# A one-core decoder step: three weight sums leave stage 1, the scalings after the mixing get a tile of their own, a batch's first weights and up's first operands change place

## The chip, the cores and the metric

One core of one Trainium2 chip runs the whole step as one program. The metric is the device time of that program in microseconds (us). TensorE (PE) does the matrix products, VectorE (DVE), ScalarE (ACT) and GpSimd (POOL) the elementwise work, and all transfers are issued by the queue of SyncE (SP). Each engine works through its own list of instructions strictly in order.

## The reference

One layer of a decoder for a prompt of 2048 positions and 8 samples of 8 positions (2112 columns, width 1024). Cut to what matters here:

```
h     = rms_norm(x, pre_mix_g)
z     = h @ w_in                      # q, k, v, sg_u, sg_v, mq, gate_logits
...                                   # three branches of width 512: windowed attention,
                                      # spatial gating, attention into 256 memory tokens
proj  = einsum('blnc,ncd->blnd', branches, w_o)
mixed = sum(sigmoid(gate_logits) * proj, axis=branch)
x     = x + rms_norm(mixed, post_mix_g)
up    = rms_norm(x, pre_ffn_g) @ w_up            # width 2 * 2816
c     = conv_b + causal convolution of width 3 over up
act   = gelu(c[:2816]) * c[2816:]
x     = x + rms_norm(act @ w_down, post_ffn_g)
```

Everything is float32, and so is the accuracy that is wanted: each operand of a product is split into a rounded part and a rest, and three products of parts (rounded with rounded, rounded with rest, rest with rounded) make one.

## The kernel before

The work lies feature-major: 128 features on the partitions, positions along the free axis. **Stage 1** (`pass_a`, 0 to about 470 us, and `pass_b`, about 470 to 714 us) makes the three branches, pair of token blocks by pair of token blocks, and writes them to the tensors `br`. **Stage 2** goes through the 2112 columns in three groups g of 704 (two halves of 352): `gate_phase` (714 to 1248 us) makes the gates, 12 jobs per group; `mix_phase` (to 1553 us) makes the output projection, with 24 products of 128 x 704 per group (3 branches n, 8 output tiles o), multiplies each by its gate and adds them up; `up_phase` (to 2467 us) has 22 jobs per group, `down_phase` the rest.

Gate, up and down use a Strassen-like scheme: a job is a 256-row block of the weights times a group, and takes 7 products of 12 matmuls (128 x 128 by 128 x 352) instead of 8. For that each job wants seven weight tiles: three blocks as they are (wa11, wa12, wa22) and four sums of blocks (ws1 to ws4). `eng.weights` loads raw blocks (`r..`, line 824), and splits them: ACT casts the rounded part (L76), DVE subtracts it to get the rest (L77). The sums are made once, by DVE (L113 in `prep_sums`, L837 where a gate job makes its own), split, written to `sum_d` (L116, L848) and read back where they are wanted. The group's columns are likewise split by `eng.operands`: 8 tiles of 704 columns are loaded (L781), scaled by norm and gain (L783), and give seven sets of four operand tiles (ob11, ot1, ob21, ot2, ob22, ot3, ot4), with differences on DVE (L793) and splits on ACT and DVE.

The sums that up needs, 22 blocks f of `w3`, are made ahead: `prep_sums` for f below NF1 = 14 runs in `pass_b`, two per item, with a pool of two buffers for the split sums; f = 14 to 21 run in gate's groups 1 and 2, in every third job. Those of down (d0 to d7) run in up.

In `mix_phase` a product `ps_p` has three buffers in PSUM. DVE evicts it, multiplied by its gate (L1038 for the first branch, into `m`; L1041 for the others, into `sl`, added to `m` by POOL, L1042). When group g is done, `post_mix` runs during group g + 1: the norm `rs` (L997), then for each of 8 tiles a scaling of `m` in place (L1004, DVE), `x` reloaded as `xr` (two buffers, L1003) and added by POOL (L1007), the sum written to `x1_d` (L1008), its square on ACT (L988) added up on DVE (L989). After the last group, `up_phase` begins with the norm of group 0 and the operands `u0`, made under `tc.high_priority(None)`, which puts them ahead of all other work that is ready.

The order on each engine is set when the program is built, by a scheduler that goes through the code with a model of the time and with priorities; code that is written earlier, or marked with a priority, is placed earlier. Tile pools of a later phase lie on memory of an earlier one, and wait for its tiles.

## Time and profile before

| | before |
|---|---|
| median of 3 runs | 2978.36 us (2975.37 to 2981.42) |
| profiled execution, its own time | 2972.76 us |
| its span | 2970.9 us |
| PE busy | 2868.4 us (97%) |
| DVE busy | 2057.4 us (69%) |
| ACT busy | 1395.8 us (47%) |
| POOL busy | 499.2 us (17%) |
| granted TensorE clock, mean | 0.984 |

The profiled execution lies 5.6 us under the median, and 1.9 us of it lie outside the span. A busy share counts an instruction from its start to its end, at whatever clock. What a stretch lost for PE is its length less its busy time weighted with the granted clock: at a clock of 0.50 (TensorE at 1.2 instead of 2.4 GHz) a busy microsecond is worth half of one.

### The profile page before, as it was taken

How to read it: one execution, taken by the hardware profiler on the slowest of the kernel's cores; microseconds unless marked ns; L12 is line 12 of the kernel's file. 1: busy time of each engine (PE TensorE's matmuls, PEld its weight loads, DVE VectorE, ACT ScalarE, POOL GpSimd, SP SyncE). 2: the span in 40 equal slices, each digit the busy share in tenths (PEclk: the TensorE clock that was granted, in tenths of full speed). 3: DMA queues.
4: the chain of work that ended last, by engine and by line, in shares of the span. 5: the costliest groups of instructions: out<-in, count | busy, mean ns of one | idle time of the engine just before them, and what ended most of it. 6: DMA issues, size and time to landing. Idle time of an engine off the chain costs nothing.

```text
span 2970.9 us, 52583 instructions
## 1 busy us (share of the span) xinstructions
PE 2868.4 (97%) x19340; PEld 2821.0 (95%) x19340; DVE 2057.4 (69%) x3901; ACT 1395.8 (47%) x2793; POOL 499.2 (17%) x576
## 2 busy tenths in 40 slices
PE   8999999996999999999999999999999999999997
PEld 8998998996999999999989999999999999999997
DVE  6676567888767353468787777867785667767667
ACT  5555556334555354423325555555554454334333
POOL 3221100010000000035552211311242121000000
PEclk9999999998999999999999999999999999999998
DMA  6123223887889999867678987898787778576674
GB/s 213 52 68 88 73 69 115 266 294 269 326 309 350 340 358 342 319 222 247 207 270 297 336 327 245 309 335 328 241 321 244 242 241 287 198 271 230 210 268 134
DMA packets 310945, 732.32 MB, mean 247 GB/s; under 512 B 37968, under 2 KB 90192, under 8 KB 310672
## 3 DMA queue, kind: packets, MB, share of 16 engines
q1 hardware_dynamic: 310688, 728.97, 70.5%
q8 instruction: 153, 2.51, 0.3%
q14 instruction: 104, 0.85, 0.1%
HBM read 553.55 MB, written 176.27 MB: 246 GB/s over the span
## 4 chain that ended last, share of the span: by engine, by line
PE 87%; DVE 4%; DMA 4%; issue 2%; ACT 2%; POOL 1%; SPq 0%; DVEq 0%; ACTq 0%; POOLq 0%
PE ps_xu L885 17%; PE ps_xg L885 9%; PE ps_yu L885 9%; PE ps_p L1029 8%; PE ps_xd L885 6%; PE ps_yg L885 5%; PE ps_p L1285 5%; PE ps_wu L885 4%; PE ps_q L215 3%; PE ps_yd L885 3%; PE ps_mqp L229 3%; PE ps_wg L885 2%; PE ps_kv L215 2%; PE ps_sv L215 2%; PE ps_wd L885 1%
## 5 line engine op out<-in xcount | busy, mean ns | idle before, releaser
L1170 DVE SCALAR_TENSOR_TENSOR c<-e,k_conv_w,c 128x704 f32<-128x704 f32 (+1 forms) x264 | 252.0, 956 | 109.6 <-ACT c L1166 104.0
L1029 PE MATMUL ps_p<-b,w_p 128*128 128x352 f32 x1728 | 285.4, 327 | 11.7 <-DVE m L1038 9.0
L1029 PEld LDWEIGHTS ps_p<-b,w_p 128*128 128x128 f32 x1728 | 281.9, 191 | 13.1 <-issue 9.5
L885 PE MATMUL ps_xu<-ot_u,ws_u 128*128 128x352 f32 x1584 | 275.3, 323 | 0.0
L885 PEld LDWEIGHTS ps_xu<-ot_u,ws_u 128*128 128x128 f32 x1584 | 257.2, 188 | 0.0
L1042 POOL TENSOR_TENSOR m<-m,sl 128x704 f32<-128x704 f32 x48 | 105.4, 2204 | 653.4 <-DMA bx<-br 574.3
L77 DVE TENSOR_TENSOR wa_u<-r_u,wa_u 128x512 fp32r<-128x512 f32 x198 | 138.8, 704 | 24.4 <-ACT wa_u L76 22.0
L1166 ACT ACTIVATE c<-e,k_conv_b,k_conv_w 128x704 f32<-128x704 f32 (+1 forms) x132 | 129.6, 982 | 50.5 <-DVE e L1145 39.5
L885 PE MATMUL ps_xg<-ot_h,ws_g 128*128 128x352 f32 x864 | 152.0, 324 | 0.0
L76 ACT CAST wa_u<-r_u 128x512 fp32r<-128x512 f32 x198 | 123.1, 624 | 61.4 <-PE ps_yu L885 44.1
L885 PE MATMUL ps_xu<-ob_u,wa_u 128*128 128x352 f32 x792 | 149.0, 323 | 0.5 <-ACT sq_m L988 0.5
L1157 POOL COPY tails<-e 128x2 f32<-128x2 f32 x88 | 71.5, 813 | 456.5 <-DVE e L1145 446.4
L885 PE MATMUL ps_yu<-ot_u,ws_u 128*128 128x352 f32 x792 | 142.8, 325 | 3.9 <-DVE sl L1041 3.9
L885 PE MATMUL ps_wu<-ob_u,wa_u 128*128 128x352 f32 x792 | 146.6, 323 | 0.0
L885 PEld LDWEIGHTS ps_xg<-ot_h,ws_g 128*128 128x128 f32 x864 | 141.5, 188 | 0.2 <-ACT ws_g L76 0.2
L1285 PE MATMUL ps_p<-a,wd 128*128 128x352 f32 x864 | 140.3, 323 | 0.3 <-DVE y L1293 0.3
L1285 PEld LDWEIGHTS ps_p<-a,wd 128*128 128x128 f32 x864 | 138.4, 188 | 0.6 <-DVE y L1293 0.6
L885 PE MATMUL ps_xu<-ot_u,wa_u 128*128 128x352 f32 x792 | 138.2, 324 | 0.0
L885 PE MATMUL ps_yu<-ob_u,ws_u 128*128 128x352 f32 x792 | 137.8, 323 | 0.0
L885 PEld LDWEIGHTS ps_yu<-ot_u,ws_u 128*128 128x128 f32 x792 | 130.8, 190 | 4.2 <-DVE sl L1041 4.2
L885 PEld LDWEIGHTS ps_xu<-ob_u,wa_u 128*128 128x128 f32 x792 | 130.4, 189 | 0.8 <-ACT sq_m L988 0.8
L885 PEld LDWEIGHTS ps_wu<-ob_u,wa_u 128*128 128x128 f32 x792 | 130.3, 188 | 0.0
(381 smaller groups left out, 6690.6 us busy)
## 6 DMA issues: line engine op xcount, KB each, us to landing
ws_u<-sum_d SPq DMA_DIRECT2D x264, 512.0 KB, 5.5
r_u<-in_w_dram SPq DMA_DIRECT2D x286, 256.0 KB, 5.1
ws_g<-sum_d SPq DMA_DIRECT2D x96, 512.0 KB, 7.7
ws_d<-sum_d SPq DMA_DIRECT2D x96, 512.0 KB, 4.5
sum_d<-ws_u SPq DMA_DIRECT2D x88, 512.0 KB, 4.0
r_g<-in_wg_dram SPq DMA_DIRECT2D x120, 256.0 KB, 5.2
r_d<-in_w4s_dram SPq DMA_DIRECT2D x104, 256.0 KB, 4.1
sg_d<-sg SPq DMA_DIRECT2D x72, 352.0 KB, 5.0
```

The source lines that it names most:

```text
L76: nc.scalar.copy(out=hi, in_=src)
L77: nc.vector.tensor_tensor(out=lo, in0=src, in1=_f(hi), op=ALU.subtract)
L215: nc.tensor.matmul(ps[:nt, :256], lhsT=h[k // 4][:, a, k % 4, c0 : c0 + nt], rhs=wv[:, b, k], start=(n == 0), stop=(n == 3 * KT - 1),)
L229: nc.tensor.matmul(ps[:, :nt], lhsT=wv[:, a, k, half * P : (half + 1) * P], rhs=h[k // 4][:, b, k % 4, :nt], start=(n == 0), stop=(n == 3 ...
L885: nc.tensor.matmul(ps[:, :CW], lhsT=ws[w][:, a, j], rhs=ops[o][j][:, b], start=(start and n == 0), stop=(n == 3 * HK - 1), skip_group_chec ...
L1029: nc.tensor.matmul(ps[:, c, :CW], lhsT=w[:, a, 4 * oo + k], rhs=bs[k][:, b, c * CW : (c + 1) * CW], start=(i == 0), stop=(i == 11),)
L1042: nc.gpsimd.tensor_tensor(out=mx[o], in0=mx[o], in1=sg, op=ALU.add)
L1157: nc.gpsimd.tensor_copy(out=tails[:, ft], in_=e[:, T2 : T2 + 2])
L1166: nc.scalar.activation(c[:, :cwid], e[:, 2:ew], AF.Identity, bias=cb[:, ft : ft + 1], scale=cw[:, ft, 2:3])
L1170: nc.vector.scalar_tensor_tensor(out=c[:, :cwid], in0=e[:, t : t + cwid], scalar=cw[:, ft, t : t + 1], in1=c[:, :cwid], op0=ALU.mult, op1= ...
L1285: nc.tensor.matmul(ps[:, :CW], lhsT=w[k // 4][:, a, k % 4], rhs=acts[k][c][:, b], start=(n == 0), stop=(n == 3 * ND - 1),)
```

## The change

There are four edits.

1. NF1 goes from 14 to 11, and NF2 = 19 is new. The sums f = 11, 12, 13 leave `pass_b`. Gate's eight slots make f = 11 to 18. The last three, f = 19, 20, 21, are made in up's group 0, behind the jobs 10, 13 and 16. The sums for down that stood in up's group 0 (behind jobs 11 and 14) move on: five stay in group 1, three stand in group 2 behind jobs 2, 5 and 8.
2. In gate, up and down the first weights of a batch are asked for ahead of the batch's operands.
3. In `post_mix` the scaling writes a tile of its own, `t` (`tm`, one buffer), instead of `m` in place, and POOL adds `t` and `x` into `m`.
4. The operands `u0` get priority 300 instead of the highest.

```diff
-NF1 = 14
+NF1, NF2 = 11, 19
...
     def jobs():
-        todo = list(range(NF1, NF))
+        todo = list(range(NF1, NF2))
...
+            ws = eng.weights(I["wg"][0], sum_d[NF], g == 0, f"g{g}_0")
             ops = eng.operands(lambda k: I["xT"][:, k, c0 : c0 + T2], f"h{g}", 0, rb)
             for i in range(12):
-                yield f"g{g}_{i}", eng.weights(I["wg"][i], sum_d[NF + i], g == 0, f"g{g}_{i}"), ops, Sink(g, i)
+                if i:
+                    ws = eng.weights(I["wg"][i], sum_d[NF + i], g == 0, f"g{g}_{i}")
+                yield f"g{g}_{i}", ws, ops, Sink(g, i)
...
+            t = xp.tile([P, T2], F32, tag="t", name=f"tm_{g}_{o}")
             nc.vector.scalar_tensor_tensor(
-                out=m, in0=m, scalar=gains[:, 2, o : o + 1], in1=rs, op0=ALU.mult, op1=ALU.mult
+                out=t, in0=m, scalar=gains[:, 2, o : o + 1], in1=rs, op0=ALU.mult, op1=ALU.mult
             )
-            nc.gpsimd.tensor_tensor(out=m, in0=m, in1=x, op=ALU.add)
+            nc.gpsimd.tensor_tensor(out=m, in0=t, in1=x, op=ALU.add)
...
-    with tc.high_priority(None):
+    with tc.high_priority(300):
         ops0 = eng.operands(lambda k: x1_d[0][k], "u0", 3, norms(acx_d[0], "0"))
...
-        preps = [(g, f) for g, fs in ((0, (11, 14)), (1, (2, 5, 8, 11, 14)), (2, (2,))) for f in fs]
+        preps = [(g, f) for g, fs in ((1, (2, 5, 8, 11, 14)), (2, (2, 5, 8))) for f in fs]
...
+                if g == 0 and f in (10, 13, 16):
+                    u = NF2 + (f - 10) // 3
+                    prep_sums(rw, wo, I["w3"][u], sum_d[u], f"u{u}")
...
             if g + 1 < NG2:
+                ws = eng.weights(I["w3"][0], sum_d[0], False, f"u{g + 1}_0")
                 ops = eng.operands(lambda k: x1_d[g + 1][k], f"u{g + 1}", 3, rb)
...
+            ws = eng.weights(I["w4s"][4 * b], sum_d[NF + 12 + 4 * b], False, f"d{g}_{b}_0")
             ops = eng.operands(lambda k: act_d[8 * b + k][:, g * T2 : (g + 1) * T2], f"d{g}_{b}", None, None)
```

Lines 1003 to 1042 of before stand three or four lines lower in the changed kernel (L1004 is L1008, L1038 is L1042, L1041 is L1045, L989 is L992, L997 is L1000).

**Place A, SP's list where gate begins.** Before, behind the last sums of stage 1 (`ws2_u12` and later); r0, r2, r3_g0_0 are the first raw blocks of gate's first job.

```order
L116 DMA sum_d12_79<-ws3_u12_8807 128x1024
L108 DMA r0_u13_8821<-in_w3_dram 128x512
L742 DMA br1_61<-ob_14_9348 128x4x128
L108 DMA r1_u13_8835<-in_w3_dram 128x512
L116 DMA sum_d13_80<-ws0_u13_8817 128x1024
L116 DMA sum_d13_80<-ws1_u13_8825 128x1024
L742 DMA br1_61<-ob_15_9357 128x4x128
L116 DMA sum_d13_80<-ws2_u13_8831 128x1024
L116 DMA sum_d13_80<-ws3_u13_8839 128x1024
L781 DMA x_h1_0_11284<-in_xT_dram 128x704
L824 DMA r0_g0_0_9546<-in_wg_dram 128x512
L824 DMA r2_g0_0_9551<-in_wg_dram 128x512
```

The same place in the changed kernel, where the last sum of stage 1 is that of f = 10:

```order
L116 DMA sum_d10_77<-ws2_u10_8466 128x1024
L116 DMA sum_d10_77<-ws3_u10_8474 128x1024
L742 DMA br1_61<-ob_12_9003 128x4x128
L824 DMA r0_g0_0_9322<-in_wg_dram 128x512
L824 DMA r2_g0_0_9327<-in_wg_dram 128x512
L824 DMA r3_g0_0_9329<-in_wg_dram 128x512
L742 DMA br1_61<-ob_13_9012 128x4x128
L824 DMA r1_g0_0_9337<-in_wg_dram 128x512
L824 DMA r0_g0_1_9581<-in_wg_dram 128x512
```

The first job's raw blocks stood behind the last of stage 1's sums and behind the last branch block, `ob_15`. Now they stand just behind `ob_12`.

**Place B, DVE's list in the mixing of group 1, around the scalings of group 0.** Before:

```order
L1038 TENSOR_TENSOR m_1_4_15983<-sl_1_0_4_15981,ps_p1_0_4_15956 128x704
L997 COPY rs_0_15948<-ps_st0_15928 128x704
L1004 SCALAR_TENSOR_TENSOR m_0_0_14995<-m_0_0_14995,c_gains_164,rs_0_15948 128x704
L1004 SCALAR_TENSOR_TENSOR m_0_1_15024<-m_0_1_15024,c_gains_164,rs_0_15948 128x704
L1004 SCALAR_TENSOR_TENSOR m_0_2_15058<-m_0_2_15058,c_gains_164,rs_0_15948 128x704
L1004 SCALAR_TENSOR_TENSOR m_0_3_15087<-m_0_3_15087,c_gains_164,rs_0_15948 128x704
L1004 SCALAR_TENSOR_TENSOR m_0_4_15121<-m_0_4_15121,c_gains_164,rs_0_15948 128x704
L1004 SCALAR_TENSOR_TENSOR m_0_5_15150<-m_0_5_15150,c_gains_164,rs_0_15948 128x704
L1004 SCALAR_TENSOR_TENSOR m_0_6_15184<-m_0_6_15184,c_gains_164,rs_0_15948 128x704
L1004 SCALAR_TENSOR_TENSOR m_0_7_15213<-m_0_7_15213,c_gains_164,rs_0_15948 128x704
L1038 TENSOR_TENSOR m_1_5_16012<-sl_1_0_5_16010,ps_p1_0_5_15985 128x704
L77 TENSOR_TENSOR w_p1_1_1_16206<-ws_p1_1_1_16207,w_p1_1_1_16206 128x1024
```

And in the changed kernel:

```order
L1042 TENSOR_TENSOR m_1_4_15887<-sl_1_0_4_15885,ps_p1_0_4_15860 128x704
L1000 COPY rs_0_15852<-ps_st0_15832 128x704
L1008 SCALAR_TENSOR_TENSOR tm_0_0_15920<-m_0_0_14899,c_gains_164,rs_0_15852 128x704
L1042 TENSOR_TENSOR m_1_5_15916<-sl_1_0_5_15914,ps_p1_0_5_15889 128x704
L77 TENSOR_TENSOR w_p1_1_1_16116<-ws_p1_1_1_16117,w_p1_1_1_16116 128x1024
L1008 SCALAR_TENSOR_TENSOR tm_0_1_15927<-m_0_1_14928,c_gains_164,rs_0_15852 128x704
L1042 TENSOR_TENSOR m_1_6_15966<-sl_1_0_6_15964,ps_p1_0_6_15939 128x704
L1008 SCALAR_TENSOR_TENSOR tm_0_2_15999<-m_0_2_14962,c_gains_164,rs_0_15852 128x704
L77 TENSOR_TENSOR b_2_0_0_16619<-bx_2_0_0_16620,b_2_0_0_16619 128x704
L992 TENSOR_TENSOR acx_0_15854<-acx_0_15854,sq_x0_1_15931 128x704
L77 TENSOR_TENSOR b_2_0_1_16624<-bx_2_0_1_16625,b_2_0_1_16624 128x704
L1042 TENSOR_TENSOR m_1_7_15995<-sl_1_0_7_15993,ps_p1_0_7_15968 128x704
```

Between two evictions there now stands one scaling, the scalings of group 0 reach as far as product 4 of the second branch, and those of group 1 lie likewise in group 2.

**Place C, DVE's list at the end of the mixing, around the eviction of product 4 of the last branch.** Before, the weights of up's first jobs (`wa..`) stand there, the scalings of `x_u0` six evictions earlier, ahead of that of `ps_p2_1_6`:

```order
L1041 TENSOR_TENSOR sl_2_2_3_17489<-sl_2_2_3_17489,ps_p2_2_3_17464 128x704
L77 TENSOR_TENSOR wa11_u0_0_17866<-r0_u0_0_17867,wa11_u0_0_17866 128x512
L77 TENSOR_TENSOR wa12_u0_0_17873<-r1_u0_0_17874,wa12_u0_0_17873 128x512
L989 TENSOR_TENSOR ac_2_16706<-ac_2_16706,sq_m2_1_17422 128x704
L1041 TENSOR_TENSOR sl_2_2_4_17527<-sl_2_2_4_17527,ps_p2_2_4_17502 128x704
```

In the changed kernel, from the same eviction on:

```order
L1045 TENSOR_TENSOR sl_2_2_3_17409<-sl_2_2_3_17409,ps_p2_2_3_17384 128x704
L992 TENSOR_TENSOR ac_2_16618<-ac_2_16618,sq_m2_2_17380 128x704
L1096 COPY rb2_0_17619<-ps_su0_1_17635 128x352
L783 SCALAR_TENSOR_TENSOR x_u0_0_17648<-x_u0_0_17648,c_gains_164,rb2_0_17619 128x704
L783 SCALAR_TENSOR_TENSOR x_u0_1_17654<-x_u0_1_17654,c_gains_164,rb2_0_17619 128x704
L783 SCALAR_TENSOR_TENSOR x_u0_2_17660<-x_u0_2_17660,c_gains_164,rb2_0_17619 128x704
L783 SCALAR_TENSOR_TENSOR x_u0_3_17666<-x_u0_3_17666,c_gains_164,rb2_0_17619 128x704
L783 SCALAR_TENSOR_TENSOR x_u0_4_17692<-x_u0_4_17692,c_gains_164,rb2_0_17619 128x704
L783 SCALAR_TENSOR_TENSOR x_u0_5_17698<-x_u0_5_17698,c_gains_164,rb2_0_17619 128x704
L783 SCALAR_TENSOR_TENSOR x_u0_6_17704<-x_u0_6_17704,c_gains_164,rb2_0_17619 128x704
L783 SCALAR_TENSOR_TENSOR x_u0_7_17710<-x_u0_7_17710,c_gains_164,rb2_0_17619 128x704
L793 TENSOR_TENSOR t_u0_0_17672<-x_u0_0_17648 128x352
```

The eight scalings of `x_u0` and four rows more come ahead of the eviction of `ps_p2_2_4`, and the operands' whole first part (scalings, ob11, ot1) stands among the evictions of the products 3 to 7. Behind the last of these, `sl_2_2_7`, ob21, ob22, ot3 and ot2 follow in both kernels. Where down's groups 0 and 1 begin, PE, DVE and ACT have the same sequence in both kernels but for a single cast.

## Rows read from the trace of the kernel before

**Rows 1.** The page: busy time, share and instructions by engine; the span and the clock.
```profile
PE 2868.4 (97%) x19340; PEld 2821.0 (95%) x19340; DVE 2057.4 (69%) x3901; ACT 1395.8 (47%) x2793; POOL 499.2 (17%) x576
...
core 0: 2970.9 us, clock 0.984
```

**Rows 2.** Stretches: length, busy PE PEld DVE ACT POOL (count), PEclk, DMA share, GB/s.
```profile
710.00:715.00 5.00, 3.92 (x34) 3.73 (x32) 4.84 (x8) 1.52 (x3) 0.87 (x2) 1.00 0.80 265
715.00:720.00 5.00, 0.00 (x0) 0.00 (x0) 2.46 (x5) 3.23 (x9) 0.00 (x0) 0.93 0.91 322
720.00:725.00 5.00, 2.08 (x8) 1.78 (x8) 5.00 (x10) 3.71 (x10) 0.00 (x0) 0.50 0.54 163
...
740.00:745.00 5.00, 3.23 (x10) 2.78 (x11) 4.90 (x9) 0.91 (x2) 0.00 (x0) 0.50 0.97 349
745.00:750.00 5.00, 2.38 (x9) 1.70 (x8) 5.00 (x8) 1.59 (x3) 0.00 (x0) 0.84 1.05 401
750.00:755.00 5.00, 3.94 (x15) 3.49 (x15) 5.00 (x9) 1.49 (x4) 0.00 (x0) 0.66 0.41 152
```

**Rows 3.** Waits of PE, 700 to 760 us; of SP's queue, 650 to 765 us.
```profile
PE ps_xg L885 <- ACT wa_g L76: 18.3, 1, 18.3
PE psg L735 <- DVE ob L739: 6.1, 1, 6.1
...
SPq L116 <- DVE ws_u L77: 41.7, 27, 4.9
```

**Rows 4.** Timeline of SP's queue, 728 to 745 us: start, length, what.
```profile
731.92 0.92 SPq L116 DMA_DIRECT2D sum_d<-ws_u  x2
...
735.96 1.37 SPq L824 DMA_DIRECT2D r_g<-in_wg_dram  x3
```

**Rows 5.** DVE's groups, 714 to 740 us: count, busy, mean ns, idle before.
```profile
L77 DVE TENSOR_TENSOR ob_h<-x_h,ob_h 128x352 fp32r<-128x352 f32 x12 | 5.7, 523 | 0.0
L77 DVE TENSOR_TENSOR ws_u<-s_u,ws_u 128x512 fp32r<-128x512 f32 x6 | 4.1, 691 | 1.8 <-ACT ws_u L76 1.8
```

**Rows 6.** Busy time by stretch again: the mixing of group 1.
```profile
1375.00:1380.00 5.00, 1.07 (x7) 0.78 (x5) 5.00 (x4) 2.40 (x3) 3.90 (x2) 0.80 0.60 199
1380.00:1385.00 5.00, 4.41 (x15) 4.44 (x16) 5.00 (x6) 0.79 (x1) 2.71 (x1) 0.51 0.62 139
```

**Rows 7.** The scalings' line (min/median/max ns); timeline: eight of them, and PE's wait.
```profile
L1004 DVE SCALAR_TENSOR_TENSOR m<-m,c_gains,rs x16: 939/1656/2415, 1366.9 to 1479.3; 128x704 f32<-128x704 f32 x16
...
1366.86 12.78 DVE L1004 SCALAR_TENSOR_TENSOR m<-m,c_gains,rs 128x704 f32<-128x704 f32 x8
...
1380.59 11.71 PE L1029 MATMUL ps_p<-b,w_p 128*128 128x352 f32 x59 [4.52 <-DVE m L1038]
```

**Rows 8.** DVE's groups, 1360 to 1400 us; POOL's, 1366 to 1400 us.
```profile
L989 DVE TENSOR_TENSOR acx<-acx,sq_x 128x704 f32<-128x704 f32 x5 | 6.6, 1318 | 0.0
L77 DVE TENSOR_TENSOR w_p<-ws_p,w_p 128x1024 fp32r<-128x1024 f32 x4 | 6.4, 1592 | 0.0
L77 DVE TENSOR_TENSOR b<-bx,b 128x704 fp32r<-128x704 f32 x4 | 5.0, 1258 | 0.0
...
L1007 POOL TENSOR_TENSOR m<-m,xr 128x704 f32<-128x704 f32 x7 | 16.8, 2415 | 14.8 <-DMA xr<-in_xT_dram 7.1 <-DVE m L1004 6.2 <-DVE m L1038 1.5
```

**Rows 9.** Waits of PE, 1240 to 1570 us, on late evictions.
```profile
PE ps_yu L885 <- DVE sl L1041: 3.9, 1, 3.9
PE ps_p L1029 <- DVE sl L1041: 2.2, 2, 1.6
```

**Rows 10.** DVE's timeline: up's first scalings, and the last eviction of the mixing.
```profile
1512.31 8.55 DVE L783 SCALAR_TENSOR_TENSOR x_u<-x_u,c_gains,rb 128x704 f32<-128x704 f32 x8
...
1558.33 0.88 DVE L1041 TENSOR_TENSOR sl<-sl,ps_p 128x704 f32<-128x704 f32 x1
```

**Rows 11.** Busy time by stretch: up's group 0, and where down's second group begins.
```profile
1575.00:1862.00 287.00, 287.00 (x1818) 286.83 (x1817) 212.28 (x317) 155.13 (x273) 63.50 (x90) 1.00 0.84 304
...
2645.00:2650.00 5.00, 1.16 (x4) 1.16 (x5) 5.00 (x7) 0.46 (x1) 0.00 (x0) 0.78 0.23 89
```

More of the change, by code (lines that the diff above doesn't have):

```diff
@@ L1199, in jobs @@
             for f in range(NF):
-                yield f"u{g}_{f}", eng.weights(I["w3"][f], sum_d[f], False, f"u{g}_{f}"), ops, Sink(g, f)
+                if f or not g:
+                    ws = eng.weights(I["w3"][f], sum_d[f], False, f"u{g}_{f}")
+                yield f"u{g}_{f}", ws, ops, Sink(g, f)
                 if (g, f) in preps:
@@ L1330, in down_phase @@
                 i, nm = 4 * b + op, f"d{g}_{b}_{op}"
-                ws = eng.weights(I["w4s"][i], sum_d[NF + 12 + i], False, nm)
+                if op:
+                    ws = eng.weights(I["w4s"][i], sum_d[NF + 12 + i], False, nm)
                 end = quad(nm, ws, ops, ys[2 * op : 2 * op + 2], b == 0, end)
```

## Prediction

> **What bounds the kernel now.** PE is busy for 97% of the span at a mean granted clock of 0.984 [rows 1], so what an edit can give is time in which PE stands or runs at the low clock. I read the stretches of five microseconds first, to find where that is, then PE's waits there, then the lists and timelines of the engines that it waits for. The loss of a stretch is its length less PE's busy time times the granted clock. Three regions bear on this change.
>
> Where gate begins, 710 to 755 us, the six stretches shown lose 1.1, 5.0, 4.0, 3.4, 3.0 and 2.4 us, and the three between them, in which no matmul ran, 15: 33.8 us together [rows 2]. The wait behind it is one of 18.3 us for the first job's first weight tile, and 6.1 us for a branch block [rows 3]. That tile was late since its raw blocks were: SP issued them at 735.96, right behind the last two writes of stage 1's sums (731.92, and these wait for DVE in their turn) [rows 4]. Over the whole passage SP stood 41.7 us in 27 waits for such sums [rows 3].
>
> In the mixing of group 1 PE loses 4.1 + 2.8 us [rows 6], and as much in that of group 2, 102 us later: 13.8 in all. Eight scalings in a row hold DVE for 12.78 us, and PE waits 4.5 us for the eviction behind them [rows 7]; the clock then falls to 0.5 [rows 6].
>
> From the mixing to up PE waits 3.9 + 2.2 = 6.1 us for evictions [rows 9]. What little it runs at a lower clock behind these I leave out.
>
> The rest lies where nothing changes: 24 us where down and its second and third group begin (one stretch of it: 1.16 busy at 0.78 [rows 11]).
>
> **Edit 1, the sums that leave stage 1.** Three sets of 4 sums and 4 splits, with 4 writes of 512 KB each, go from the stretch in which gate's first blocks wait behind them. In place A the raw blocks then stand behind `ob_12` instead of behind 8 further writes, so they are there when stage 1's last matmuls end at about 714. From there DVE's work sets the pace. Two jobs need 14 splits and 8 sums at 0.69 us (I take the duration of the same tile size, `ws_u`, 691 ns [rows 5]) = 15.2 us; group 0's operands need 28 splits and 16 differences at 5.7/12 = 0.48 us [rows 5] = 21 us. With a few branch blocks (3 us) that is 39 us; some 2 us of operands were done ahead before, as they can be now, so DVE is through at about 751. PE has 2 jobs of 84 matmuls at 0.16 us (287 us for 1818 [rows 11]) = 27 us in that time; it can start at about 721 with a cold clock and so is not what ends last. The two jobs end at 751 plus a last product of about 2 us, 753 to 754. Before, by the 755 mark, 34 matmuls had run (10 + 9 + 15 [rows 2]), which is 5.4 us of work, and PE ran on at full speed: the two jobs ended at 755 + 27 - 5.4 = 776.6. The gain is **22 us**. From below: if DVE stands as often as now (1.8 us in 26 us behind one line [rows 5], and up to 10 us for late blocks) it is 12; from above, if 4 us more of the operands are made ahead, 26.
>
> The sums have to be made elsewhere. Gate's eight slots are the same in number. In up's group 0 three sets stand in place of two, in group 2 three in place of one. DVE has 212 of 287 us there and PE stands for none of it [rows 11]; a set costs DVE 8 x 0.69 = 5.5 us, which leaves it under 77%. Cost 0; if DVE's slack were not to be had where it falls, 5.5 us for each of three sets more, 16 us.
>
> **Edit 2, weights first.** In gate's first group this helps the casts `wa11` to stand ahead of the operands' and is part of the 22. In down and at up's later groups the lists at the begins are the same as before, so 0; the 24 us stay.
>
> **Edit 3, the scalings.** In place B an eviction follows each scaling. The scaling of tile o + 1 must now wait until POOL has added tile o, since `t` has one buffer, and the adds (2.4 us each [rows 8]) wait for `xr`. What is queued behind a waiting scaling is the next eviction, and behind that PE. A product is 24 matmuls, 3.9 us, and with three PSUM buffers an eviction may end 7.7 us after the end of its product. From the norm to the eviction of the second branch's product 5 DVE has 8 scalings at 1.66 us, 7 adds of squares at 1.32 [rows 7, 8], 9 evictions at 0.88 [rows 10], 5 weight splits at 1.59 and 4 branch splits at 1.26 [rows 8], 43.5 us: from 1366.9 on the last eviction ends at 1410. PE had the first branch done at 1380.59 - 4.52 = 1376.1 [rows 7]; six products more end at 1399.2, and their eviction may end at 1399.2 + 7.7 = 1407. So some 3 us of stalls would stay in each of the two groups by these durations, in pieces, and less where fewer adds of POOL lie beside them; I take 2, and no low clock for stalls so short. Of 6.9 us in each group I take 5: **10 us**. The ends are 13.8 (no stall left) and 0 (stalls as long as now).
>
> What the trace shows of the scalings themselves is that the same instruction takes from 0.94 to 2.4 us, median 1.66, beside POOL's adds [rows 7]. The Trainium skill, SBUF — State Buffer, "Who interferes with whom", says that a VectorE instruction with two inputs in SBUF and a GpSimd instruction that reads SBUF exclude each other, the one that starts second waiting. The spread agrees with that in kind. By that rule the new order helps once more, since a scaling and its own add take turns: at 0.94 us each DVE has 5.8 us less to do, no stall is left, and the sum would be 4 us lower.
>
> **Edit 4, up's operands later.** In place C the eight scalings (8.55 us [rows 10]) and some 12 differences and splits now stand between the evictions of the last five products. From the eviction of product 3 to that of product 7 DVE has about 21 us; PE runs those four products in 15.4 us, and up's second product (`ps_yu`, 2 us behind the first) waits for the last eviction. So PE stands about 4 us around the begin of up, where it waited 6.1 before: **2 us** gained, because the earlier stalls in the mixing go and the later one stays. The ends: a gain of 6, and a loss of 3 if the norm's result comes late.
>
> **Sum.** 22 + 10 + 2 = 34 us. Against the profiled execution's own time 2972.8 - 34 = 2938.8; that execution lay 5.6 us under the median, so 2944 us.
>
> **The rivals.** First, gate's begin stays paced by late blocks or casts, with a gain of 10 to 12 instead of 22: 2954 to 2956. For it speaks that the splits lie on memory of stage 1's weights and can't start before its last matmul, so PE idles from 714 anyhow and restarts at the low clock; against it, that 33.8 us are lost now and most of that behind one SP queue.
>
> Second, the one buffer of `t`: a scaling that waits for POOL, which waits for `xr` (7.1 us of its idle time went there [rows 8]), holds the evictions. From a chain of more than 3.9 us per tile on, each further tile costs what exceeds it; at 5 us that is 9 us per group less what the slack of 7.7 covers, and with the 2 us above and the low clock some 5 us: no gain from edit 3, 2954, or a little above. Against it: add and scaling together are 2.4 + 1.66 = 4.1 us, just above the limit.
>
> Third, up's operands come so late that PE stands 9 to 12 us instead of 4: 2949 to 2952.
>
> Fourth, on the other side: the sums in up hold SP's queue. 12 writes stand in group 0 instead of 8, and 12 instead of 4 in group 2. Each can hold SP for up to 4.9 us [rows 3], and behind it stand the weights of coming jobs; 12 writes more at 4.9 are 59 us, which gives 3003. It decides from the point where the weights are later than the one job of 13.5 us that they are asked for ahead. Against it stands that group 0 has 8 such writes now and PE waits for nothing.
>
> Fifth, it does more: gate's 26, 13.8 in the mixing and 6 at up, 2932, or something at down's begins on top.
>
> That the change doesn't do what it says is excluded by places A to C, except edit 2 in up and down, where it does nothing.
>
> **How the numbers follow.** The forecast of 2944 (2936 to 2950) has a chance of 0.52; the first rival 0.16, the second 0.12, the third 0.07, the first three together (2972 and up, about no change) 0.03, the fourth 0.04, the fifth 0.06. The range is 2929 to 2960: it holds the forecast, the fifth, and the first three each alone with some microseconds more. About 0.2%, 6 us, is what a measurement of this kernel can tell from no change. Faster 0.93, the same 0.03, slower 0.04.
>
> **What would show it.** In the profile after: no wait of over 8 us at gate's begin, first gate matmul at about 721, full speed from about 740 instead of 755, and PE's waits in 710 to 760 on DVE's operands; in the mixing no PE wait for `m` above 2 us and no clock at 0.5; the scalings apart, each behind an add of POOL; a wait for `sl` of 3 to 5 us at up's begin; DVE 1 to 3% busier in up, PE with no wait there. Wrong it would be if the first gate matmul came after 730, if scalings waited over 2 us each for POOL, or if up showed waits for `ws_u`.

## The result, and the profile after

| | before | after |
|---|---|---|
| median of 4 runs | 2976.96 us (2975.37 to 2981.42) | 2955.47 us (2953.11 to 2958.40) |
| ratio, 95% interval | | 0.9926 (0.9909 to 0.9943) |
| profiled execution, its own time | 2972.76 us | 2958.40 us |
| its span | 2970.9 us | 2956.6 us |

The change makes the kernel faster by 21.5 us. The forecast was 2944 us, a gain of 34: sign and range hold, but the time is 11.5 us above the forecast, and outside the 2936 to 2950 that the forecast gave itself. After's profiled execution is the slowest of its four, and before's lies below all four of its own, so the two profiles differ by only 14.3 us.

I take the loss of PE as the prediction does (length less busy time times granted clock) and add it up by region, from stretches of five microseconds:

| region | before | after | gain forecast | gain seen |
|---|---|---|---|---|
| begin of gate | 33.8 | 9.0 | 22 | 24.8 |
| mixing, groups 1 and 2 | 13.7 | 7.0 | 10 | 6.7 |
| mixing to up | 7.9 | 11.4 | 2 | -3.5 |
| inside up | 0.0 | 0.8 | 0 | -0.8 |
| begin of down | 3.7 | 15.2 | 0 | -11.5 |
| all else | 66.3 | 64.9 | 0 | 1.4 |

The gains add up to 17.1 us, 2.8 more than the spans differ by: that is how rough this count is. What stretches at the edge of a region lose, where it is 0.4 us or less, stands in the last row.

The page's first line and the clock, which answer to [rows 1]:

```profile
PE 2872.3 (97%) x19340; PEld 2821.9 (95%) x19340; DVE 2048.9 (69%) x3901; ACT 1395.4 (47%) x2793; POOL 487.6 (16%) x576
...
core 0: 2956.6 us, clock 0.986
```

Stretches of after (columns as in [rows 2]): the begin of gate, the mixing of groups 1 and 2, the begin of up, and the begin of down:

```profile
715.00:720.00 5.00, 1.94 (x10) 1.13 (x8) 5.00 (x10) 5.00 (x12) 0.00 (x0) 0.82 0.74 264
720.00:725.00 5.00, 4.41 (x14) 4.14 (x15) 5.00 (x12) 4.30 (x10) 0.00 (x0) 0.50 0.97 333
725.00:730.00 5.00, 5.00 (x33) 5.00 (x32) 5.00 (x11) 2.87 (x7) 0.00 (x0) 0.99 0.54 171
...
1380.00:1385.00 5.00, 4.16 (x27) 3.90 (x26) 5.00 (x4) 1.94 (x3) 4.11 (x3) 1.00 0.88 304
...
1490.00:1495.00 5.00, 3.08 (x16) 3.08 (x17) 1.18 (x3) 1.28 (x2) 3.51 (x3) 0.81 0.72 257
...
1525.00:1530.00 5.00, 0.00 (x0) 0.00 (x0) 5.00 (x8) 4.04 (x9) 1.89 (x1) 0.72 0.25 99
...
2450.00:2455.00 5.00, 3.89 (x12) 3.43 (x12) 2.06 (x5) 0.50 (x2) 0.00 (x0) 0.50 1.04 413
2455.00:2460.00 5.00, 0.30 (x1) 0.30 (x2) 0.00 (x0) 0.80 (x3) 0.00 (x0) 0.50 0.90 352
```

PE's waits in after, in three passages: 700 to 760 us, 1360 to 1570 us and 2400 to 2470 us (sum, times, longest). They answer to [rows 3, 9]:

```profile
PE ps_xg L885 <- ACT ob_h L76: 1.6, 1, 1.6
...
PE ps_yu L885 <- ACT sq_m L991: 6.6, 1, 6.6
PE ps_p L1033 <- DVE sl L1045: 4.8, 5, 1.8
PE ps_su L98 <- POOL rstd_u L95: 2.6, 1, 2.6
PE ps_yu L885 <- DMA ws_u<-sum_d: 1.3, 1, 1.3
...
PE ps_yd L885 <- ACT y L1245: 5.3, 1, 5.3
PE ps_xd L885 <- ACT wa_d L76: 1.7, 1, 1.7
PE ps_xd L885 <- ACT y L1245: 1.1, 1, 1.1
```

At gate's begin the wait of 18.3 us is gone, and the clock is back at 0.99 from 725 us on. In the mixing no wait for an eviction is over 1.8 us. Four waits are new or longer:

- 2.6 us in the mixing of group 2 (1489.3 to 1491.9), for POOL's step of the norm that `u0` needs (`rstd_u`). It stood behind two adds that held POOL for 4.91 us from 1485.99 on.
- 6.6 us at up's begin; in the stretch from 1525 us on PE does nothing at all. The row names a square on ACT, but the last eviction of the mixing ends at 1530.45 us and PE goes on at 1530.56.
- 1.3 us soon after it for a tile `ws_u`. SP issued it at 1546.28, behind the store of a sum of squares that DVE had finished at 1545.85, and so not behind the sums that edit 1 brings into up, which come with job 10.
- 5.3 us where down begins, with the clock at 0.50 on both sides.

In before PE's waits at down's begin were 1.7, 1.1 and 0.9 us, and the row for `ps_yd` was not there.

### The profile page after: what moved, and what is told of

Its sections match the earlier page's. It is cut to its first block, busy times and chain, and to the rows that moved or that the text cites. A ratio compares the mean times of both kernels' runs of the same rounds, so it can differ in the third digit from the quotient of the medians.

```text
span 2956.6 us, 52536 instructions
## 1 busy us (share of the span) xinstructions
PE 2872.3 (97%) x19340; PEld 2821.9 (95%) x19340; DVE 2048.9 (69%) x3901; ACT 1395.4 (47%) x2793; POOL 487.6 (16%) x576
## 5 line engine op out<-in xcount | busy, mean ns | idle before, releaser
L1046 POOL TENSOR_TENSOR m<-m,sl 128x704 f32<-128x704 f32 x48 | 96.6, 2019 | 632.9 <-DMA sl<-sg_d 553.7
```

The costliest lines, as they stand in the source:

```text
L1046: nc.gpsimd.tensor_tensor(out=mx[o], in0=mx[o], in1=sg, op=ALU.add)
```

## The experiments

Twelve kernels, each with its ratio to before from runs on the same chip. A difference of 0.2% is about what such a comparison resolves. The regions named are those of the table above.

### Each edit by itself

Edit 1 in before, alone:

```diff
-NF1 = 14
+NF1, NF2 = 11, 19
```

(with the loops over `NF2` and the moved sums as in the change.)

> The kernel before with edit 1 alone (the sums 11 to 13 out of stage 1, 19 to 21 in up). Theory: gate's begin loses about 9 us instead of 33.8, since the raw blocks no longer stand behind the writes of the sums: 2977 - 25 = 2952, all else as before. Rival (the casts of the first weights have to stand ahead of the operands', edit 2): a gain of 10 to 15 only, 2962 to 2967, with PE waiting for ACT's casts at gate's begin. Third possibility, the sums in up cost something: PE would wait there, where it waits for nothing now.

Measured: 2952.83 us, ratio 0.9927 (0.9913 to 0.9942). That is the gain of the whole change, with one edit of four. The begin of gate loses 9.1 us instead of 33.8, the first gate matmul starts at 718.0 us, and inside up PE loses nothing. Down's begin loses 9.3 us instead of 3.7, with two waits for `y` of 2.8 us together.

Edit 2 in before, alone:

```diff
+            ws = eng.weights(I["wg"][0], sum_d[NF], g == 0, f"g{g}_0")
             ops = eng.operands(lambda k: I["xT"][:, k, c0 : c0 + T2], f"h{g}", 0, rb)
...
```

(and likewise in up and down, as in the change.)

> The kernel before with edit 2 alone (a batch's first weights asked for ahead of its operands). Theory: nothing; the raw blocks still stand behind the sums' writes at gate's begin, and the lists of up and down hardly change: within 3 us of before, gate's begin still loses 33 to 37 us. Rival (edit 2 carries a part of the gain at gate's begin): 5 us or more off there, 2970 or less.

Measured: 2975.60 us, 0.9998 (0.9989 to 1.0008): nothing. The begin of gate loses 33.9 us, and PE waits there 18.0 us for the first weight tile, as in [rows 3].

Edit 3 in before, alone:

```diff
+            t = xp.tile([P, T2], F32, tag="t", name=f"tm_{g}_{o}")
...
-                out=m, in0=m, scalar=gains[:, 2, o : o + 1], in1=rs, op0=ALU.mult, op1=ALU.mult
+                out=t, in0=m, scalar=gains[:, 2, o : o + 1], in1=rs, op0=ALU.mult, op1=ALU.mult
...
-            nc.gpsimd.tensor_tensor(out=m, in0=m, in1=x, op=ALU.add)
+            nc.gpsimd.tensor_tensor(out=m, in0=t, in1=x, op=ALU.add)
```

> The kernel before with edit 3 alone (the scalings write a tile t of their own). Theory: the two stalls of 4.5 us with the low clock behind them (13.7 us) turn into several short waits of under 1 us, 7 us in all as in the changed kernel: 2977 - 6.7 = 2970. Rival (7 us of waits came from edit 4, whose operands lie in the same stretch): no waits stay, 2977 - 13.7 = 2963. Durations of the scalings: about 0.94 us where no add of POOL runs, about 2.4 where one does, if the two exclude each other.

Measured: 2977.95 us, 1.0016 (1.0006 to 1.0025): no gain, if anything a little slower. DVE's timeline in the mixing of group 2, and PE's wait there, 1400 to 1570 us:

```profile
1504.12 8.43 DVE L783 SCALAR_TENSOR_TENSOR x_u<-x_u,c_gains,rb 128x704 f32<-128x704 f32 x8
1512.90 0.88 DVE L1042 TENSOR_TENSOR sl<-sl,ps_p 128x704 f32<-128x704 f32 x1
...
1515.71 2.38 DVE L1005 SCALAR_TENSOR_TENSOR tm<-m,c_gains,rs 128x704 f32<-128x704 f32 x1
...
PE ps_p L1030 <- DVE sl L1042: 8.3, 5, 4.1
```

Group 1 loses 2.9 us instead of 6.9. In group 2 the spread scalings now share their place with the eight of `x_u0`, and 8.6 us are lost: the bunch that edit 3 takes apart is replaced by another. Mixing and begin of up together give 3.8 us back (17.8 against 21.6); the begins of gate and down take 3.2 and 7.7 in this profile, the latter with 4.3 us of waits for `y`. So the edit alone is no gain, for a reason inside the mixing and one outside it.

Edit 4 taken out of after:

```diff
-    with tc.high_priority(300):
+    with tc.high_priority(None):
```

> The changed kernel with edit 4 alone undone (the operands u0 at the highest priority again). In the changed kernel PE loses 11.4 us between the end of the mixing and up (7.9 before), and 15.6 us where down begins (3.7 before). Theory: the first is edit 4, the second is memory: ACT's copy of the second tile y of down waits for the store of up's last block, on whose memory y_0_1 came to lie; in this variant y_0_1 waits for DVE alone. Then the begin of up loses about 8 again and that of down about 4: 3.5 + 11.5 = 15 us less than the changed kernel's 2955.5, about 2940. Rival (the loss at down is the two sets of sums that came into up's last group, or a matter of one execution): it stays, and only 3.5 us are gained, 2952.

Measured: 2949.76 us, 0.9917 (0.9900 to 0.9933), where I had expected 2940. Against after's ratio (0.9926) the times alone don't tell the two apart; the profile does. Up's begin loses 4.8 us instead of 11.4, and group 2 of the mixing 8.9 instead of 4.0, for the reason just seen (its stretch, and PE's waits from 1400 to 1570 us):

```profile
1480.00:1485.00 5.00, 2.65 (x17) 2.35 (x15) 5.00 (x7) 1.05 (x1) 0.00 (x0) 1.00 0.08 30
...
PE ps_p L1033 <- DVE sl L1045: 6.1, 2, 4.1
PE ps_yu L885 <- DVE sl L1045: 3.5, 1, 3.5
```

Edit 4 moves a stall of some 5 us from the mixing to up's begin and makes it no shorter (6.6 us lost there against 4.9 gained). In this kernel the begin of down loses 7.9 us, not 15.2: its wait for `y` is 1.1 us, as in before.

### The new wait where down begins

PE waits there for ACT to evict a product into `y`. ACT's timeline, and the store in SP's timeline, in after:

```profile
2450.05 0.45 ACT L1245 COPY y<-ps_xd 128x352 f32<-128x352 f32 x1
2459.20 0.45 ACT L1245 COPY y<-ps_yd 128x352 f32<-128x352 f32 x1 [8.70 <-DMA act_d<-e]
...
2452.12 0.33 SPq L1197 DMA_DIRECT2D act_d<-e  x1
```

ACT stands 8.70 us for a store of up's output. The `y` tiles lie on memory of up's tiles `e`; in after the second `y` lies on the `e` of up's last block, whose store is issued at 2452.12 and lands seven microseconds later. In before the same eviction waited 1.34 us, for the store of the block ahead of it. The instructions of PE, DVE and ACT there have the same order in both kernels; what differs, by the releasers of these waits, is which tile's memory is taken. The next kernel exchanges two pools of down, which lays `y` elsewhere:

```diff
-    yp, sp = pool(c2, "yd", 10), pool(c2, "sd", 1)
+    sp, yp = pool(c2, "sd", 1), pool(c2, "yd", 10)
```

> The changed kernel, where down's pools of y and of its small tiles change places, so that no y tile lies on memory of up's last stores. Theory: PE's 5.3 us wait for ACT's copy of y, and the low clock on both sides of it, go: down's begin loses about 4 us instead of 15.6, the begin of up still 11.4; 2955.5 - 11.5 = 2944. Rival (the loss comes from late loads behind the sums in up's last group): PE waits as long, for ws_d or wa_d instead, and the time stays at 2953 to 2957.

Measured: 2950.17 us, 0.9915 (0.9900 to 0.9930), where I had expected 2944. The wait for `y` is 3.0 us instead of 5.3 + 1.1, and the begin of down loses 7.1 us instead of 15.2. By the ratios that is 3 us less than after, but the two intervals overlap: it is shown by the profile, not by the times alone. Up's begin still loses 12.7.

Edits 1 and 2 with the pools exchanged (edits 3 and 4 left out):

```diff
-    with tc.high_priority(300):
+    with tc.high_priority(None):
...
-                out=t, in0=m, scalar=gains[:, 2, o : o + 1], in1=rs, op0=ALU.mult, op1=ALU.mult
+                out=m, in0=m, scalar=gains[:, 2, o : o + 1], in1=rs, op0=ALU.mult, op1=ALU.mult
```

> Edits 1 and 2, without 3 and 4, and with down's two pools exchanged, so that no y tile lies on memory of up's last stores. Theory: the 22 us of edit 1 alone (2952.8), less the 5 us that the wait of ACT for the last store still cost there: gate's begin loses 9, the mixing 13 and 8 as before, down's begin 4: 2947 to 2948. This beats the changed kernel if edits 3 and 4 together bring nothing. Rival (edit 3 is worth its 6 us in the mixing also here): 2953, with down's begin as in the run with edit 1 alone.

Measured: 2954.58 us, 0.9932 (0.9914 to 0.9949), some 7 us above what I expected. The begin of down loses 8.1 us, with waits of 1.7, 1.6 and 0.9: nearly those of before, which lost 3.7. The waits are not what is left there; the clock is (last section). And 3.8 us went inside up, behind a wait of 2.5 us for POOL's step of a norm (`rstd_u`).

### Why the scalings cost what they cost

The rival for edit 3 was the single buffer of `t`. Edits 1 to 3 with two:

```diff
-            t = xp.tile([P, T2], F32, tag="t", name=f"tm_{g}_{o}")
+            t = xp.tile([P, T2], F32, tag="t", name=f"tm_{g}_{o}", bufs=2)
```

> As the run with edit 4 undone, and the tile t with two buffers instead of one. Theory (the short waits in the mixing come from DVE's work as a whole and from the exclusion of POOL's adds): the waits stay within 1 us of those with one buffer (2.9 us in group 1, about 8 at the begin of group 2's second branch); 2948 to 2951. Rival (the one buffer makes the scalings wait for POOL, 9.2 us in 8 waits, and holds the evictions): 4 to 8 us of waits go, 2942 to 2946.

Measured: 2954.66 us, 0.9938 (0.9922 to 0.9955): no gain. The kernel to set beside it is after without edit 4 (0.9917), which differs in this one buffer alone. The scalings' lines of the two (min/median/max ns), first with one buffer, then with two:

```profile
L1008 DVE SCALAR_TENSOR_TENSOR tm<-m,c_gains,rs x16: 940/952/2387, 1339.5 to 1488.5; 128x704 f32<-128x704 f32 x16
```

```profile
L1008 DVE SCALAR_TENSOR_TENSOR tm<-m,c_gains,rs x16: 937/946/2425, 1341.2 to 1472.8; 128x704 f32<-128x704 f32 x16
```

DVE's waits for POOL ahead of the scalings are 3.5 us with one buffer and 3.8 with two; the 9.2 us of my expectation are those of after, with edit 4. PE's waits for `sl` in the mixing are 9.0 and 7.8 us. So the single buffer is not the cause. The order of the instructions changes which of them are long (in after the scalings' median is 1664 ns), but not their sum: the seven groups that DVE has in the mixing (weight and branch splits, both kinds of eviction, scalings, both sums of squares) take 218.1 us in before, 216.7 in after, 219.7 without edit 4 and 220.1 with two buffers, in counts that differ by one. What one kind of instruction is spared, another pays. That leads to POOL. DVE's and POOL's timelines in after, 1360 to 1370 us (start, length, what; in brackets the engine's idle time before and what ended it), and the scalings' line (min/median/max ns), which answers to [rows 7]:

```profile
1360.92 2.39 DVE L1008 SCALAR_TENSOR_TENSOR tm<-m,c_gains,rs 128x704 f32<-128x704 f32 x1
1363.24 0.88 DVE L992 TENSOR_TENSOR acx<-acx,sq_x 128x704 f32<-128x704 f32 x1
1364.04 0.87 DVE L1045 TENSOR_TENSOR sl<-sl,ps_p 128x704 f32<-128x704 f32 x1
1364.84 1.96 DVE L77 TENSOR_TENSOR w_p<-ws_p,w_p 128x1024 fp32r<-128x1024 f32 x1
1366.72 2.38 DVE L1008 SCALAR_TENSOR_TENSOR tm<-m,c_gains,rs 128x704 f32<-128x704 f32 x1
...
1360.28 2.29 POOL L1046 TENSOR_TENSOR m<-m,sl 128x704 f32<-128x704 f32 x1 [1.62 <-DVE sl L1045]
1363.45 2.26 POOL L1011 TENSOR_TENSOR m<-tm,xr 128x704 f32<-128x704 f32 x1 [0.88 <-DMA xr<-in_xT_dram]
1365.68 2.67 POOL L1046 TENSOR_TENSOR m<-m,sl 128x704 f32<-128x704 f32 x1
...
L1008 DVE SCALAR_TENSOR_TENSOR tm<-m,c_gains,rs x16: 939/1664/2392, 1341.8 to 1479.3; 128x704 f32<-128x704 f32 x16
```

The scaling at 1360.92 starts while POOL adds (1360.28 to 1362.57) and ends 0.74 us after that add; the one at 1366.72 ends 0.75 us after the add that ends at 1368.35. So each seems to do its work once POOL is through. The add of squares at 1363.24 started ahead of POOL's next add and takes its plain 0.88, and the eviction at 1364.04, which reads PSUM and one tile of SBUF, takes 0.87 beside a running add. At 1365.68 it is POOL that waits: its add takes 2.67 us, and the split that started before it ends at 1366.80. This is what the Trainium skill, SBUF — State Buffer, "Who interferes with whom", says: a VectorE instruction with two inputs in SBUF and a GpSimd instruction that reads SBUF exclude each other. The rows agree, with 0.94 us free and 2.39 held. Many of the adds in the way are not the scalings' own (L1011) but those that add `sl` to `m` (L1046), 48 of them.

So: edits 1 to 3, the pools exchanged, and these 48 adds on DVE.

```diff
-                        nc.gpsimd.tensor_tensor(out=mx[o], in0=mx[o], in1=sg, op=ALU.add)
+                        nc.vector.tensor_tensor(out=mx[o], in0=mx[o], in1=sg, op=ALU.add)
```

> As the run with edit 4 undone and down's pools exchanged, and the adds of the gated branches to m (sl to m, 48 of them at 2.0 us on POOL) are made on DVE instead. Theory (a DVE instruction with two inputs in SBUF and an add of POOL exclude each other): what DVE's scalings, adds of squares and splits lose to those adds (up to 1.45 us each) goes, and they take 0.94, 0.88 and 1.2 us nearly throughout, but for those beside the 16 adds of x that stay on POOL; against that DVE has 48 adds at 0.88 = 42 us more in 300. The waits in the mixing then are as many or fewer: 2942 to 2950. Rival (no exclusion, just slower memory): the durations stay spread, DVE has 42 us more, PE waits 10 us more in the mixing, 2960.

Measured: 2945.23 us, 0.9902 (0.9888 to 0.9917). Inside up this kernel loses 7.0 us, at two waits (3.6 us together) for POOL's step of a later group's norm (`rstd_u`), with the clock down to 0.52 behind the longer one; in after PE does not wait there. The mixing loses 1.7 + 1.8 us, and all sixteen scalings take the same time:

```profile
L1008 DVE SCALAR_TENSOR_TENSOR tm<-m,c_gains,rs x16: 939/946/953, 1343.0 to 1484.6; 128x704 f32<-128x704 f32 x16
```

The same with edit 4 back in (priority 300):

> The run with the adds to m on DVE (2945.2), with edit 4 put back (priority 300): all four edits, DVE's adds and down's pools exchanged. It prices edit 4 alone where nothing else disturbs. Theory: the eight scalings of x_u0 and the splits come among the last five evictions, and PE waits 5 to 8 us in all around the begin of up instead of 2 to 3: 2949 to 2952. Rival (in the changed kernel that loss came from POOL's adds that hold DVE, not from the place of the operands): the same within 2 us, 2944 to 2947.

Measured: 2938.03 us, 0.9881 (0.9866 to 0.9896), below both of my readings. By the total edit 4 costs nothing here, but the profile shows that its stall has stayed:

```profile
PE ps_yu L885 <- ACT sq_m L991: 4.7, 1, 4.7
```

The region from the mixing to up loses 7.1 us, where the kernel without edit 4 loses about 4, and group 2 of the mixing nothing instead of 1.8. What makes the total lower are the 7.0 us of the other kernel inside up, at its waits for the norm, which are not met here; that edit 4 removes them is not shown.

The kernel with 48 adds on DVE, without edit 4, and POOL's other 16 adds (those of `x`) on DVE too:

```diff
-            nc.gpsimd.tensor_tensor(out=m, in0=t, in1=x, op=ALU.add)
+            nc.vector.tensor_tensor(out=m, in0=t, in1=x, op=ALU.add)
```

> As the run with the adds to m on DVE, and the 16 adds of x after the scalings go to DVE too, so that POOL adds nothing in the mixing. Theory (exclusion): the adds of squares, still 1.69 us at the mean beside the adds of x, go to 0.9; DVE has 16 x 0.88 = 14 us more and saves about as much; PE's waits in the mixing stay within 2 us of those with the adds of x on POOL: 2943 to 2947. Rival (DVE is then simply full): 5 us or more of waits in the mixing, 2950.

Measured: 2935.55 us, 0.9870 (0.9855 to 0.9885), below the expected 2943 to 2947. The mixing loses 0.3 us instead of 3.5. Inside up it loses 0.4 instead of 7.0: the waits for the norm are not met here either, which the expectation had no term for.

The same without edit 3, the scalings in place and in a row of eight as in before:

```diff
-                out=t, in0=m, scalar=gains[:, 2, o : o + 1], in1=rs, op0=ALU.mult, op1=ALU.mult
+                out=m, in0=m, scalar=gains[:, 2, o : o + 1], in1=rs, op0=ALU.mult, op1=ALU.mult
```

> As that, and edit 3 undone: the eight scalings stand in a row again, in place, but no add of POOL runs beside them. It parts the two causes of the stall of 4.5 us in the kernel before: the row of eight, and their 1.6 us each. Theory (the exclusion makes the row too long): the row takes 8 x 0.94 = 7.5 us instead of 12.78, which the three PSUM buffers cover (7.7 us), so at most 1 us of stall per group is left and the time is that of the run before within 2 us, 2944 to 2948. Rival (a row of eight is too long in itself): a stall of 2 to 4 us in each group and the low clock behind it, 2950 to 2956.

Measured: 2935.53 us, 0.9870 (0.9853 to 0.9886), the best, level with the last kernel; by the ratios (0.9870 against 0.9926) it is some 17 us below after. PE's one wait in the mixing is 0.9 us, beside bunched scalings:

```profile
L1007 DVE SCALAR_TENSOR_TENSOR m<-m,c_gains,rs x16: 944/947/952, 1339.7 to 1441.1; 128x704 f32<-128x704 f32 x16
...
PE ps_p L1032 <- DVE sl L1044: 0.9, 1, 0.9
```

So the bunching by itself was not the cause of the stalls; with POOL out of the way, unbunching is worth nothing. The kernel with edits 1 and 2 and the pools exchanged (0.9932) differs from this one in the 64 adds alone: by the ratios they are worth 18 us.

Last, the cause by itself: before, with its 64 adds of the mixing on DVE and nothing else changed.

```diff
-            nc.gpsimd.tensor_tensor(out=m, in0=m, in1=x, op=ALU.add)
+            nc.vector.tensor_tensor(out=m, in0=m, in1=x, op=ALU.add)
...
-                        nc.gpsimd.tensor_tensor(out=mx[o], in0=mx[o], in1=sg, op=ALU.add)
+                        nc.vector.tensor_tensor(out=mx[o], in0=mx[o], in1=sg, op=ALU.add)
```

> The kernel before, with one thing changed: all adds of the mixing (x after the scalings, the gated branches to m) are on DVE instead of POOL. Theory (a DVE instruction with two inputs in SBUF waits out a POOL add, and that made the row of eight scalings 12.78 us long): the row takes 7.0 to 7.6 us, the two stalls of 4.5 us with the low clock behind them go, as does most of the 6 us of late evictions towards up; the mixing loses 5 to 8 us instead of 21.6, so 13 to 17 us off: 2957 to 2961, and gate's begin still loses 34. Rival (in the runs with edit 1 the gain came from the changed order, not from POOL): within 5 us of before.

Measured: 2954.78 us, 0.9941 (0.9924 to 0.9958): 18 to 19 us by moving work onto the busier engine. The eight scalings still stand in a row, which takes 6.99 us instead of 12.78 [rows 7]. DVE's groups over the mixing (count, busy, mean ns, idle before), first in before, then in this kernel, with its row of eight ahead:

```profile
L77 DVE TENSOR_TENSOR w_p<-ws_p,w_p 128x1024 fp32r<-128x1024 f32 x34 | 56.0, 1646 | 4.4 <-ACT w_p L76 3.9 <-DMA ws_p<-in_wp_dram 0.2
L1004 DVE SCALAR_TENSOR_TENSOR m<-m,c_gains,rs 128x704 f32<-128x704 f32 x16 | 25.5, 1665 | 0.1
```

```profile
1365.46 6.99 DVE L1004 SCALAR_TENSOR_TENSOR m<-m,c_gains,rs 128x704 f32<-128x704 f32 x8
...
L1042 DVE TENSOR_TENSOR m<-m,sl 128x704 f32<-128x704 f32 x47 | 41.7, 887 | 0.4
L77 DVE TENSOR_TENSOR w_p<-ws_p,w_p 128x1024 fp32r<-128x1024 f32 x33 | 40.3, 1221 | 1.7 <-ACT w_p L76 1.3 <-issue 0.3
L1007 DVE TENSOR_TENSOR m<-m,xr 128x704 f32<-128x704 f32 x16 | 14.2, 885 | 0.6 <-DMA xr<-in_xT_dram 0.6
L1004 DVE SCALAR_TENSOR_TENSOR m<-m,c_gains,rs 128x704 f32<-128x704 f32 x16 | 14.0, 947 | 0.1
```

64 adds of 0.89 us are 57 us more for DVE. The seven groups of the mixing that DVE had before fall from 218.1 to 171.4 us at the same time (in counts that differ by three at the passage's ends), so that its load there grows by only 9 us. PE's loss in the mixing falls from 13.7 to 0.0 and at up's begin from 7.9 to 5.6; these 16 us are most of the 18.6 between the two profiles.

The two causes add up: 0.9927 (edit 1) times 0.9941 (adds on DVE) is 0.9868, and the two kernels with both, which hold edit 2 and the exchanged pools besides, measure 0.9870.

## Why the prediction was right or wrong

**What bounds the kernel: right.** PE's lost time was in the regions named, and the largest gain came out of the largest of them.

**Edit 1, 22 us: right, by the working.** Gate's begin gives 24.8 us in the profile, between the forecast 22 and the upper end 26. The first gate matmul starts at 717.5 us where 721 was said, the clock is full from 725 instead of 740, and PE's waits are for operands, at most 1.6 us each. The first rival (blocks and casts as late as before) is out: e3_sums_only shows the gain with edit 1 alone. SP's 41.7 us at stage 1's sums [rows 3] are 24.3 us in 14 waits.

**Its sums in up, cost 0: right.** PE loses 0.8 us inside up in after and 0.0 in the kernel with edit 1 alone; the fourth rival (59 us by SP's queue) is out. The one wait for `ws_u`, which the prediction named as a sign of being wrong, is 1.3 us and has another origin, as said above.

**Edit 2, 0 by itself: right**, shown by e5_first_only. That it is part of the 22 in gate's first group was wrong: gate's begin loses 9.1 us without it (e3_sums_only) and 9.0 with it.

**Edit 3, 10 us: mis-sized.** 6.7 us were gained in the mixing of after, 3.9 in group 1 and 2.8 in group 2, where 5 each was said. The sum of DVE's work (43.5 us) took the held durations of [rows 7, 8] as fixed prices, so a stall of about 3 us per group came out, which is what group 1 shows (3.0 left). In group 2 some 2.5 of the 4.0 that are left stand at the wait for `rstd_u`, which the sum had only as the lower end of edit 4. The step that failed is "less where fewer adds of POOL lie beside them": the scalings were held as much as before (1666 ns at the mean, 1665 before). The further deduction, that a scaling and its own add take turns and the scalings fall to 0.94 us, failed for the same reason: the 48 other adds take no turns with it. Without edit 4 half of the scalings do take 0.95 us or less, but other instructions grow by as much. The rule of the Trainium skill was right, and I drew too little from it: by it POOL's adds make the very stall that edit 3 was to cure, and the cure for that is another one. The second rival (one buffer of `t`) is refuted by e7_t_two_buffers.

**Edit 4, 2 us: wrong in sign.** PE stands 6.6 us at up's begin, not 4, and the region loses 3.5 us more than before, just beyond the lower end (-3). The order was read rightly: the last eviction comes behind up's first differences and splits. The term that was too small is DVE's time from the eviction of product 3 to that of product 7: 25.5 us (1504.93 to 1530.45) where 21 was said. Three short instructions in it took 5.3 us together instead of three times 0.51, and POOL's adds ran beside all three (DVE's timeline, then POOL's):

```profile
1520.77 1.24 DVE L793 TENSOR_TENSOR x_u<-x_u,x_u 128x352 f32<-128x352 f32 x1
1521.93 2.03 DVE L77 TENSOR_TENSOR ot_u<-t_u,ot_u 128x352 fp32r<-128x352 f32 x1
...
1525.56 1.99 DVE L793 TENSOR_TENSOR x_u<-x_u,x_u 128x352 f32<-128x352 f32 x1
...
1517.94 5.64 POOL L1046 TENSOR_TENSOR m<-m,sl 128x704 f32<-128x704 f32 x2 [9.77 <-DVE sl L1045]
1525.28 1.89 POOL L1046 TENSOR_TENSOR m<-m,sl 128x704 f32<-128x704 f32 x1 [1.69 <-DVE sl L1045]
```

With these adds on DVE (e9_adds_on_dve_prio300) the same stretch takes 21.2 us (1496.34 to 1517.51), though DVE makes three adds more in it, and PE waits 4.7. So the order makes a wait of about the predicted size, and POOL's adds make it longer.

**Down's begins, 0: wrong, and the largest miss.** "The lists at the begins are the same as before, so 0" compares instructions. The lists were the same, and one instruction in them waited for another store than before: 11.5 us of loss, of which 5.3 are the wait and most of the rest is the low clock around it. Exchanging two pools takes 8 of these back. Part of the miss comes with edit 1 alone, in which down's begin loses 5.6 us more than in before.

**The sum.** In the profiles 34 forecast stand against 17.1 placed: 2.8 more at gate, 3.3 less in the mixing, 5.5 less at up's begin, 11.5 less at down's, and small change. The medians differ by 21.5, not by the profiles' 14.3: before's profiled execution lies 4.2 us under the median of its four (the forecast had added 5.6, from three), and after's lies 2.9 above its own. Edits 2 to 4 together gave nothing, as e3_sums_only against after shows (0.9927 and 0.9926); by the sum they should have given 12.

**That the range held is in part luck.** 2955 is where the first and the second rival stood (2954 to 2956, and 2954 or a little above), and neither of them happened: gate's begin gave more than forecast, and the buffer of `t` cost nothing. The time came there by misses at three other places, and the largest, at down's begin, stood in the sum as zero, with no rival that made it worse.

What stays open: after's profile is of its slowest run, and which part of down's 15.2 us the other three share isn't known.

## What to carry to other kernels

When an instruction on one engine takes 0.94 us at one time and 2.39 at another, find what runs beside the long ones before re-ordering anything: here adds moved from a mostly idle engine to the busy one paid more than the careful spreading of what they hindered. A term of zero because "the order is the same" needs the waits compared too, down to which tile's memory each new tile takes over. And when several edits come together, price each for what it does alone and beside the others: two of these traded one stall for another. To judge one of them by a run, set it beside the run that differs in nothing else.

## What the runs showed of the hardware

In the mixing DVE and POOL take turns, by whole instructions, whichever comes first: a DVE instruction with two inputs in SBUF at 0.51, 0.88, 0.94 or 1.22 us free took up to 2.0, 2.4, 2.4 and 2.7 us held, and a POOL add of 128x704, 1.66 us at its shortest, up to 3.7 in after. Evictions from PSUM stayed at 0.87 to 0.89 in before and after.

TensorE's clock does not follow from the length of a wait alone. Where down begins, PE waits 1.7, 1.1 and 0.9 us both in before and in the kernel with edit 4 taken out. The stretches with these waits, first of before, then of that kernel:

```profile
2465.00:2470.00 5.00, 3.44 (x22) 3.15 (x20) 3.89 (x8) 2.01 (x4) 3.78 (x4) 1.00 0.96 293
2470.00:2475.00 5.00, 2.89 (x14) 2.31 (x15) 4.67 (x9) 1.73 (x4) 0.00 (x0) 1.00 1.03 403
```

```profile
2440.00:2445.00 5.00, 2.38 (x12) 1.80 (x11) 3.88 (x8) 2.20 (x3) 1.50 (x3) 0.87 0.98 325
2445.00:2450.00 5.00, 3.94 (x14) 3.48 (x13) 4.27 (x9) 2.27 (x6) 0.00 (x0) 0.50 1.04 412
```

In the first the granted clock stays at 1.00 and the region loses 3.7 us; in the second it falls to 0.50, the lower level, and the region loses 7.9. Why it falls in the one and not in the other was not settled.
